# First shift and scale of a two-block transformer: one route for all feature tiles, as rows on TensorE in four column groups

## The chip, the cores and the metric

The kernel runs on one core of one Trainium2 chip. The metric is device time of one launch in microseconds. It is an fp32 kernel of batch 1 with 256 tokens and 1024 features, so nearly all of its 224 MB of traffic is weights, read once.

## The reference, cut to what matters

Two transformer blocks run one after the other. The change touches only the very first step of the first one: a modulated norm of the tokens `x` (256 of them, the stream s = 0) and of the context tokens `ctx` (256, the stream s = 1), and the projection `w_in` behind it.

```python
sc, scc = silu(c), silu(c_ctx)                       # one vector of 1024 for each stream
mod   = split(sc  @ w_mod[0] + b_mod[0], 6)           # shift1, scale1, gate1, shift2, scale2, gate2
mod_c = split(scc @ w_mod[0][:, :6*D] + b_mod[0], 6)
hn = rms_norm(ctx, g_norm1[0]) * (1 + mod_c[1]) + mod_c[0]
xn = rms_norm(x,   g_norm1[0]) * (1 + scale1)   + shift1
p, pc = xn @ w_in[0], hn @ w_in[0]                    # 1024 -> 1536
```

So shift1 and scale1 are two products of a 1024-vector with a 1024x2048 slice of `w_mod` (8 MB), for two streams that share the weights. No projection of the first layer can begin on a feature tile before shift and scale of that tile are known. The other four parts of `mod`, and all of the second layer's, are needed later and are worked out in the background.

## The kernel before, in words

**Layout.** Activations lie features on partitions: `XC` holds eight feature tiles k = 0 to 7 of 128 features by 512 columns (256 of x, 256 of ctx). Every large product is made of three matmuls on operands split into a high part (a cast to fp32r) and a low part (the remainder): `mm3` issues hi*hi (L273), lo*hi (L274) and hi*lo (L275). Activations are split into `AH` and `AL`, weights into `wh` (a cast on ACT, L243) and `wl` (a subtraction on DVE, L245; for the second half tile of all it is on Pool, by `SPH`).

**The weight stream.** Weights come in half tiles of 128x1024 f32 (512 KB) in a fixed order, `halves`. `dma_to(i)` issues loads up to half i on SP's queue into a ring of four `raw` buffers (L231); `split_to(i)` splits up to half i into a ring of four `wh`/`wl`; `done(...)` moves the stream on. `ld["lim"]` holds the stream back at the start. Halves 0 and 1 hold w_in's rows for k = 0 to 3 of the first four output tiles, halves 2 and 3 those for k = 4 to 7.

**The first stage.** The four output tiles `p_c` (four PSUM banks, 96 matmuls of 512 columns over the eight k) are accumulated k by k in `in0_k(k)`: scale and shift a tile (into `n0`, the profile's `n`), cast to `AH`, subtract for `AL`, then 12 matmuls. The rms factor of each column comes from squares on ACT (L309 to L314), adds on DVE (L315), matmuls with a vector of ones (`p_ss`, L440), a power on Pool (L299), and four transposes that spread it over the partitions (`p_rb`, L444, the tile `rb`).

Shift and scale reach `modv` by two routes:

- Tiles k = 0 to 3 (`KP = 4`): the columns are packed on the host as `wmod0`, eight loads of 512 KB (`rawm`, ring of `WRB = 4`, L425). 16 fp32 matmuls of 512 columns (L431), with the two silu vectors `scf` as a 128x2 stationary operand, give two rows `p_mod`; the rows are copied (`row`, L456) and transposed in pieces back to partitions (`p_modt`, L459); four adds and two scalings on DVE give `modv` (L464, L466).
- Tiles k = 4 to 7: `st_tile` loads a transposed tile of w_mod (`wms`, 512 KB, L491, ring of `WSB = 5`) for each of scale and shift. DVE multiplies it by `scb[:, 0]` with a sum along the row (L494), Pool multiplies it by `scb[:, 1]` (L493), ACT sums that product (L496), and a small DVE operation adds the bias (L499 for scale, L501 for shift). `scb` is the silu vectors spread over the partitions by 16 transposes (`p_scb`, L372, copied out at L373). It is used later too, by `mod_bg`, which works out the remaining parts in the background (L402, L404).

**Order.** SP's instructions stand in the order in which the program writes them. Those of the other engines are put in order by a planner that simulates the timeline at build time, so an instruction can be placed ahead of work that stands before it in the program; each engine then runs its own list strictly in order. Such a piece is `cdg`, 16 diagonal matrices that ACT makes for the convolution of the first layer (L570). After the first stage come `p_q` and the rest of the projection (L289 to L291), and the buffers of the first stage are closed (`sctx.close()`); the loads of the next pool (`sm`, L528) wait for that. Three fp32 products further on serve as comparison below: `p_fa` (L761, Fourier mixer), and `p_o` (L734) and `p_bo` (L1213), the products with V in the attention of the first and second block, where two heads write to PSUM partitions 0 to 63 and 64 to 127 in turn, each with a stationary operand of 64 columns.

Of the kernel before, what the change touches and what calls it, by code (L numbers as in the profile page):

```python
# [31 lines left out]
D = 1024  # L32
# [11 lines left out]
WRB, WSB, N0B = 4, 5, 2  # L44
KP = 4
XAT = (0, 1, 1, 2)
RWP, XR0 = 0, 2
# [107 lines left out]
def tile_kernel(ctx, tc, xin, pk_d, rows_d, lc_d, bc_d, wmod0, wmod, win, wout, wfi, wfo, wsm, win2, wproj, wout2,  # L155
# [206 lines left out]
    scf = cpool.tile([128, KT, 2], F32, name="scf")  # L362
# [5 lines left out]
    for s in range(2):  # L368
        for a in range(2):
            p = psm("p_scb")  # L370
            for k in range(4):
                PE.transpose(p[:, 128 * k:128 * k + 128], scf[:, 4 * a + k, s:s + 1].to_broadcast([128, 128]), ident)  # L372
            (S.copy if a else V.tensor_copy)(scb[:, s, 512 * a:512 * a + 512], p)  # L373
# [45 lines left out]
    nj = KP // 2  # L419
    ps = [pmm("p_mod") for _ in range(nj)]  # L420
    raws = []
    for k in range(KT):
        raw = spool.tile([128, 256 * KP], F32, tag="wr", name="rawm", bufs=WRB)
        raws.append(raw)
        SP.dma_start(raw, wmod0[k])  # L425
        for i, at in enumerate(XAT):
            if at == k:
                SP.dma_start(XC[:, 2 * i:2 * i + 2], xin[:, 2 * i:2 * i + 2])
    for k in range(KT):
        for j in range(nj):  # L430
            PE.matmul(ps[j][:2], scf[:, k, :], raws[k][:, 512 * j:512 * j + 512], start=k == 0, stop=k == KT - 1)  # L431
# [3 lines left out]
    dma_to(2)  # L435
    ld["lim"] = 2
    p = psm("p_ss")
    for i in range(4):
        for n, ss in enumerate(ss_t["ss"]):
            PE.matmul(p[:, i:i + 1], ss[:, 128 * i:128 * i + 128], ones, start=n == 0, stop=n == 1)  # L440
    r = rsqrt(p[:, :4], 4, 1.0 / D, True)
    rb = psm("p_rb")
    for i in range(4):
        PE.transpose(rb[:, 128 * i:128 * i + 128], r[:, i:i + 1].to_broadcast([128, 128]), ident)  # L444
    bm1 = cpool.tile([128, KT], F32, name="bm1")
    V.tensor_scalar(bm1, P("bmod0", 8, 8), 1.0, None, op0=OP.add)
    xr = [None] * KT
    for k in range(0, XR0, 2):
        x2 = spool.tile([128, 2, 512], F32, tag="wr", name="xr", bufs=WRB)
        for i in range(2):  # L450
            V.tensor_tensor(x2[:, i], XC[:, k + i], rb, op=OP.mult)
            xr[k + i] = x2[:, i]
# [60 lines left out]
    for k in range(KT):  # L513
        in0_k(k)
# [977 lines left out]
```

## Time and profile before

| | |
|---|---|
| median of three runs | 1382.05 us (1381.72 to 1387.13) |
| the profiled execution's own time | 1382.44 us |
| its span, first to last instruction | 1380.7 us |
| mean granted TensorE clock | 0.987 of full speed |
| busy share of the span: PE, DVE, ACT, POOL | 97%, 67%, 45%, 21% |
| HBM traffic | 221 MB read, mean 161 GB/s |

The profiled execution lies 0.4 us above the median and 1.7 us above its own span. The busy share of PE counts modelled ends of pipelined matmuls, so it isn't TensorE at its peak. PE is matmul, PEld weight loads, DVE VectorE, ACT ScalarE, POOL GpSimd, SP the engine that issues most loads. An fp32 matmul appears as two records, an fp32r matmul or a transpose as one.

### The profile page before, as it was taken

What the parts mean: (1) busy time and instruction counts of PE and PEld (TensorE: products, weight loads), DVE (VectorE), ACT (ScalarE), POOL (GpSimd) and SP (SyncE); (2) the same over time, 40 slices, a digit from 0 to 9 for tenths busy, and PEclk for the clock granted to TensorE, in tenths of its full rate; (3) what the DMA queues carried; (4) which work ended last, traced back from release to release, by engine and by line L of the source; (5) the groups of instructions that cost most, each with busy time, mean ns of one, the idle gap of its engine ahead of it and who ended that gap; (6) DMA issues with size and microseconds to landing.
All of it is one profiled execution on the core that took longest, in us unless ns stands there. A gap on an engine that the chain in (4) does not pass through costs nothing.

```text
span 1380.7 us, 23081 instructions
## 1 busy us (share of the span) xinstructions
PE 1336.6 (97%) x9000; PEld 1190.3 (86%) x9000; DVE 921.3 (67%) x1597; ACT 616.5 (45%) x1030; POOL 284.6 (21%) x302
## 2 busy tenths in 40 slices
PE   6699999999999999999999999999999999999997
PEld 2595668888888888889799999999999999999997
DVE  4987999899883333349676666666555657755553
ACT  5533533423232322335565554455665455544452
POOL 2524535134420000123430000110200002322211
PEclk9799999999999999999999999999999999999999
DMA  8442453477874222344135555665335244545463
GB/s 324 138 129 75 168 169 122 159 266 252 307 282 152 92 92 67 102 139 135 51 116 190 183 184 154 183 245 185 108 120 174 105 146 176 179 172 183 155 198 107
DMA packets 66477, 223.77 MB, mean 162 GB/s; under 512 B 7488, under 2 KB 8640, under 8 KB 66368
## 3 DMA queue, kind: packets, MB, share of 16 engines
q1 hardware_dynamic: 53824, 178.16, 38.3%
q10 hardware_dynamic: 12080, 42.50, 8.9%
q0 software_dynamic: 464, 1.64, 0.3%
q8 instruction: 70, 1.15, 0.3%
q14 instruction: 39, 0.32, 0.1%
HBM read 221.22 MB, written 1.05 MB: 161 GB/s over the span
## 4 chain that ended last, share of the span: by engine, by line
PE 89%; DVE 6%; issue 2%; ACT 1%; POOL 1%; DMA 1%; SPq 0%; DVEq 0%; POOLq 0%; ACTq 0%
PE p_dn L273 6%; PE p_dn L275 6%; PE p_dn L274 6%; PE p_ua L273 4%; PE p_ua L274 4%; PE p_ug L274 4%; PE p_ua L275 4%; PE p_ug L275 4%; PE p_ug L273 4%; PE p_wo L273 2%; PE p_wo L274 2%; PE p_wo L275 2%; PE p_bq L289 2%; PE p_bq L290 2%; PE p_bq L291 2%; PE p_ga L275 2%
## 5 line engine op out<-in xcount | busy, mean ns | idle before, releaser
L245 DVE TENSOR_TENSOR wl<-raw,wh 128x1024 fp32r<-128x1024 f32 (+2 forms) x340 | 390.0, 1149 | 280.6 <-ACT wh L243 280.0
L243 ACT CAST wh<-raw 128x1024 fp32r<-128x1024 f32 (+1 forms) x344 | 332.0, 973 | 314.4 <-PE p_dn L274 90.5
L275 PE MATMUL p_dn<-HH,wl 128*128 128x256 f32 (+1 forms) x550 | 171.7, 312 | 0.5 <-DVE wl L245 0.5
L273 PE MATMUL p_dn<-HH,wh 128*128 128x256 f32 (+1 forms) x550 | 171.8, 313 | 0.0
L274 PE MATMUL p_dn<-HL,wh 128*128 128x256 f32 (+1 forms) x550 | 171.6, 312 | 0.0
L315 POOL TENSOR_TENSOR ss<-ss,sq 128x256 f32<-128x256 f32 (+1 forms) x43 | 49.2, 1144 | 435.0 <-ACT sq L314 290.4
L274 PE MATMUL p_ua<-AL,wh 128*128 128x258 f32 (+2 forms) x368 | 121.8, 331 | 3.4 <-DVE AL L341 3.4
L275 PE MATMUL p_ug<-AH,wl 128*128 128x258 f32 (+2 forms) x368 | 121.9, 331 | 0.0
L273 PE MATMUL p_ua<-AH,wh 128*128 128x258 f32 (+2 forms) x368 | 121.9, 332 | 0.0
L274 PE MATMUL p_ug<-AL,wh 128*128 128x258 f32 (+2 forms) x368 | 121.8, 331 | 0.0
L273 PE MATMUL p_ug<-AH,wh 128*128 128x258 f32 (+2 forms) x368 | 121.7, 331 | 0.0
L275 PE MATMUL p_ua<-AH,wl 128*128 128x258 f32 (+2 forms) x368 | 121.6, 330 | 0.0
L275 PEld LDWEIGHTS p_dn<-HH,wl 128*128 128x128 f32 x550 | 104.3, 190 | 6.7 <-DVE wl L245 0.7
L273 PEld LDWEIGHTS p_dn<-HH,wh 128*128 128x128 f32 x550 | 104.3, 190 | 6.2 <-ACT wh L243 0.2
L274 PEld LDWEIGHTS p_dn<-HL,wh 128*128 128x128 f32 x550 | 104.3, 190 | 6.1
L404 DVE SCALAR_TENSOR_TENSOR wm<-wm,scb 128x1024 f32<-128x1024 f32 x80 | 99.9, 1252 | 12.0 <-DMA wm<-in_wmod 11.3
L274 PEld LDWEIGHTS p_ua<-AL,wh 128*128 128x128 f32 x368 | 69.4, 188 | 10.9 <-DVE AL L341 3.8
L273 PEld LDWEIGHTS p_ug<-AH,wh 128*128 128x128 f32 x368 | 69.2, 188 | 7.3
L275 PEld LDWEIGHTS p_ua<-AH,wl 128*128 128x128 f32 x368 | 69.3, 188 | 7.1
L274 PEld LDWEIGHTS p_ug<-AL,wh 128*128 128x128 f32 x368 | 69.4, 188 | 7.0
L273 PEld LDWEIGHTS p_ua<-AH,wh 128*128 128x128 f32 x368 | 69.2, 188 | 7.1
L275 PEld LDWEIGHTS p_ug<-AH,wl 128*128 128x128 f32 x368 | 69.3, 188 | 7.0
(376 smaller groups left out, 3397.4 us busy)
## 6 DMA issues: line engine op xcount, KB each, us to landing
raw<-in_wfi SPq DMA_DIRECT2D x88, 512.0 KB, 3.8
raw<-in_win SPq DMA_DIRECT2D x84, 512.0 KB, 3.9
wm<-in_wmod ACTq DMA_DIRECT2D x80, 512.0 KB, 4.5
raw<-in_wgu SPq DMA_DIRECT2D x44, 512.0 KB, 3.7
raw<-in_wout SPq DMA_DIRECT2D x24, 512.0 KB, 3.7
raw<-in_wfo SPq DMA_DIRECT2D x32, 384.0 KB, 3.1
raw<-in_wfo SPq DMA_DIRECT2D x32, 320.0 KB, 3.3
raw<-in_wdn SPq DMA_DIRECT2D x16, 384.0 KB, 3.1
```

Of the source, the lines that this page charges most:

```text
L243: S.copy(h[:, :n], raw[:, :n])
L245: (G if every and j % every == 0 else V).tensor_tensor(lo[:, :n], raw[:, :n], h[:, :n].bitcast(F32), op=OP.subtract)
L273: PE.matmul(ps, w[0], a[0], start=first, stop=False, **kw)
L274: PE.matmul(ps, w[0], a[1], start=False, stop=False, **kw)
L275: PE.matmul(ps, w[1], a[0], start=False, stop=last, **kw)
L289: PE.matmul(ps, a[0], w[0], start=k == 0, stop=False)
L290: PE.matmul(ps, a[0], w[1], start=False, stop=False)
L291: PE.matmul(ps, a[1], w[0], start=False, stop=k == KT - 1)
L315: (eng or G).tensor_tensor(ss[0][:, cs], ss[0][:, cs], sq[:, :n], op=OP.add)
L404: V.scalar_tensor_tensor(w, w, 1.0, scb[:, 0], op0=OP.mult, op1=OP.mult, accum_out=modv[:, l, part, 0, k:k + 1])
```

## The change

All eight feature tiles now go over TensorE, in four pairs of tiles (`mod_pair(g)`). The host packs `wmod0` as 4 pairs by 4 loads of 512 KB, each load with two of the eight contraction tiles and, for each, the pair's 512 columns (256 of shift, 256 of scale). The 512 columns are cut in four: column group c of the array, 32 columns wide, makes the products of columns 128c to 128c+127, into PSUM partitions 32c to 32c+31. For that `scf` is padded with zeros from 2 to 32 columns. So a pair is 32 fp32 matmuls of 128 columns, then one copy of 128x128, one transpose, and four small DVE operations that serve both streams. `st_tile` is gone, with its eight products on DVE, eight on Pool and eight sums on ACT; so are `bm1` and the fused form in `in0_k` (scale and rms in one DVE operation for each stream): now one DVE product by the rms factor for both streams, then scale and shift on ACT, for all k.

`XC` is loaded first, ahead of all of `wmod0`. `LOADS = "mhmhmm"` gives the order behind it on SP: a pair (m), two weight halves (h), a pair, two halves, two pairs; `in0_k` follows as soon as its pair and its halves have been issued. The ring of `rawm` has 8 buffers instead of 4. The spreading of `scb` (`scb_fill`) stands at the end of the stage in the program.

```diff
@@ -41,10 +41,8 @@
 UW = T + 2 * POOL_PAD
 
 RAW, WB, EV, NT, PTB, PEB, WMB = 4, 4, 4, 2, 2, 2, 4
-WRB, WSB, N0B = 4, 5, 2
-KP = 4
-XAT = (0, 1, 1, 2)
-RWP, XR0 = 0, 2
+WRB, XRB, N0B = 8, 4, 2
+LOADS = "mhmhmm"
 NPE = 8
 CVD, FOD = 0.9, 1
 BG0, BG1 = 2.4, 2.0
@@ -359,18 +357,21 @@
     lctx = ctx.enter_context(ExitStack())
     lpool = lctx.enter_context(tc.tile_pool(name="lp", bufs=1))
     modv = cpool.tile([128, 2, 6, 2, KT], F32, name="modv")
-    scf = cpool.tile([128, KT, 2], F32, name="scf")
+    scf = cpool.tile([128, KT, 32], F32, name="scf")
+    G.memset(scf, 0.0)
     for s in range(2):
         S.activation(scf[:, :, s], P("c", 8 * s, 8), AF.Silu)
     scb = lpool.tile([128, 2, D], F32, name="scb")
     lc = lpool.tile([128, LC_W], F32, name="lc")
 
-    for s in range(2):
-        for a in range(2):
-            p = psm("p_scb")
-            for k in range(4):
-                PE.transpose(p[:, 128 * k:128 * k + 128], scf[:, 4 * a + k, s:s + 1].to_broadcast([128, 128]), ident)
-            (S.copy if a else V.tensor_copy)(scb[:, s, 512 * a:512 * a + 512], p)
+    def scb_fill():
+
+        for s in range(2):
+            for a in range(2):
+                p = psm("p_scb")
+                for k in range(4):
+                    PE.transpose(p[:, 128 * k:128 * k + 128], scf[:, 4 * a + k, s:s + 1].to_broadcast([128, 128]), ident)
+                (S.copy if a else V.tensor_copy)(scb[:, s, 512 * a:512 * a + 512], p)
 
     def mv(l, part, s):
         return modv[:, l, part, s]
@@ -416,102 +417,82 @@
 
     sctx = ctx.enter_context(ExitStack())
     spool = sctx.enter_context(tc.tile_pool(name="st", bufs=1))
-    nj = KP // 2
-    ps = [pmm("p_mod") for _ in range(nj)]
-    raws = []
-    for k in range(KT):
-        raw = spool.tile([128, 256 * KP], F32, tag="wr", name="rawm", bufs=WRB)
-        raws.append(raw)
-        SP.dma_start(raw, wmod0[k])
-        for i, at in enumerate(XAT):
-            if at == k:
-                SP.dma_start(XC[:, 2 * i:2 * i + 2], xin[:, 2 * i:2 * i + 2])
-    for k in range(KT):
-        for j in range(nj):
-            PE.matmul(ps[j][:2], scf[:, k, :], raws[k][:, 512 * j:512 * j + 512], start=k == 0, stop=k == KT - 1)
+    for i in range(4):
+        SP.dma_start(XC[:, 2 * i:2 * i + 2], xin[:, 2 * i:2 * i + 2])
     new_ss(True)
     for k in range(KT):
         sq_acc(k, slice(0, 512), k == 0, V)
-    dma_to(2)
-    ld["lim"] = 2
-    p = psm("p_ss")
-    for i in range(4):
-        for n, ss in enumerate(ss_t["ss"]):
-            PE.matmul(p[:, i:i + 1], ss[:, 128 * i:128 * i + 128], ones, start=n == 0, stop=n == 1)
-    r = rsqrt(p[:, :4], 4, 1.0 / D, True)
-    rb = psm("p_rb")
-    for i in range(4):
-        PE.transpose(rb[:, 128 * i:128 * i + 128], r[:, i:i + 1].to_broadcast([128, 128]), ident)
-    bm1 = cpool.tile([128, KT], F32, name="bm1")
-    V.tensor_scalar(bm1, P("bmod0", 8, 8), 1.0, None, op0=OP.add)
-    xr = [None] * KT
-    for k in range(0, XR0, 2):
-        x2 = spool.tile([128, 2, 512], F32, tag="wr", name="xr", bufs=WRB)
-        for i in range(2):
-            V.tensor_tensor(x2[:, i], XC[:, k + i], rb, op=OP.mult)
-            xr[k + i] = x2[:, i]
-    pt = psm("p_modt")
-    for j in range(nj):
+
+    def first_rms():
+        p = psm("p_ss")
+        for i in range(4):
+            for n, ss in enumerate(ss_t["ss"]):
+                PE.matmul(p[:, i:i + 1], ss[:, 128 * i:128 * i + 128], ones, start=n == 0, stop=n == 1)
+        r = rsqrt(p[:, :4], 4, 1.0 / D, True)
+        rb = psm("p_rb")
+        for i in range(4):
+            PE.transpose(rb[:, 128 * i:128 * i + 128], r[:, i:i + 1].to_broadcast([128, 128]), ident)
+        return rb
+
+    def mod_pair(g):
+
+        p = psm("p_mod")
+        for q in range(4):
+            raw = spool.tile([128, 2, 512], F32, tag="wr", name="rawm", bufs=WRB)
+            SP.dma_start(raw.rearrange("p i n -> p (i n)"), wmod0[g, q])
+            for i in range(2):
+                k = 2 * q + i
+                for c in range(4):
+                    PE.matmul(p[32 * c:32 * c + 32, :128], scf[:, k], raw[:, i, 128 * c:128 * c + 128], start=k == 0,
+                              stop=k == KT - 1)
         row = wk.tile([128, 512], F32, tag="ev", name="row", bufs=EV)
-        S.copy(row[:2], ps[j][:2])
-        for b in range(4):
-            o = 2 * (4 * j + b)
-            PE.transpose(pt[:, o:o + 2], row[:2, 128 * b:128 * b + 128], ident[:2, :2])
-    ptv = pt[:, :4 * KP].rearrange("p (a k s) -> p a k s", a=2, s=2)
-    for part in (1, 0):
-        for s in range(2):
-            d = modv[:, 0, part, s, 0:KP]
-            V.tensor_tensor(d, ptv[:, part, :, s], P("bmod0", part * 8, KP), op=OP.add)
+        S.copy(row[:, :128], p[:, :128])
+        pt = psm("p_modt")
+        PE.transpose(pt[:, :128], row[:, :128], ident)
+        v = pt[:, :128].rearrange("p (a k x) -> p a x k", a=2, x=32)
+        for part in (1, 0):
+            d = modv[:, 0, part, :, 2 * g:2 * g + 2]
+            V.tensor_tensor(d, v[:, part, 0:2], P("bmod0", part * 8 + 2 * g, 2)[:, None, :].to_broadcast([128, 2, 2]),
+                            op=OP.add)
             if part == 1:
-                V.scalar_tensor_tensor(d, d, 1.0, P("g1_0", 0, KP), op0=OP.add, op1=OP.mult)
+                V.scalar_tensor_tensor(d, d, 1.0, P("g1_0", 2 * g, 2)[:, None, :].to_broadcast([128, 2, 2]), op0=OP.add,
+                                       op1=OP.mult)
+
     n_ = "in0"
     ps4 = [pmm("p_c") for _ in range(4)]
 
     def in0_k(k):
+        x = spool.tile([128, 512], F32, tag="xr", name="xr", bufs=XRB)
+        V.tensor_tensor(x, XC[:, k], rb, op=OP.mult)
         t = spool.tile([128, 512], F32, tag="n0", name="n0", bufs=N0B)
-        if xr[k] is None and k % 2 == 0:
-            x2 = spool.tile([128, 2, 512], F32, tag="wr", name="xr", bufs=WRB)
-            xr[k], xr[k + 1] = x2[:, 0], x2[:, 1]
         for s in (0, 1):
             c = slice(256 * s, 256 * s + 256)
-            if k < XR0:
-                S.activation(t[:, c], xr[k][:, c], AF.Identity, bias=mv(0, 0, s)[:, k:k + 1],
-                             scale=mv(0, 1, s)[:, k:k + 1])
-            else:
-                V.scalar_tensor_tensor(xr[k][:, c], XC[:, k, c], mv(0, 1, s)[:, k:k + 1], rb[:, c], op0=OP.mult,
-                                       op1=OP.mult)
-                S.activation(t[:, c], xr[k][:, c], AF.Identity, bias=mv(0, 0, s)[:, k:k + 1])
+            S.activation(t[:, c], x[:, c], AF.Identity, bias=mv(0, 0, s)[:, k:k + 1], scale=mv(0, 1, s)[:, k:k + 1])
         S.copy(AH[:, k, 0:512], t)
         V.tensor_tensor(AL[:, k, 0:512], t, AH[:, k, 0:512].bitcast(F32), op=OP.subtract)
         for m in range(4):
             mm3(ps4[m], wk256(n_, m // 2, k, 128 * (m % 2)), act(k, slice(0, 512)), k == 0, k == KT - 1)
 
-    def st_tile(part, k):
-        w = spool.tile([128, D], F32, tag="wms", name="wms", bufs=WSB)
-        SP.dma_start(w, wmod[0, 8 * part + k])
-        jg = spool.tile([128, D], F32, tag="jgs", name="jgs", bufs=2)
-        G.tensor_tensor(jg, w, scb[:, 1], op=OP.mult)
-        V.scalar_tensor_tensor(w, w, 1.0, scb[:, 0], op0=OP.mult, op1=OP.mult,
-                               accum_out=modv[:, 0, part, 0, k:k + 1])
-        S.activation(jg, jg, AF.Copy, accum_out=modv[:, 0, part, 1, k:k + 1])
-        d = modv[:, 0, part, :, k]
-        if part == 1:
-            V.tensor_scalar(d, d, bm1[:, k:k + 1], P("g1_0", k), op0=OP.add, op1=OP.mult)
+    ld["lim"] = 0
+    rb = None
+    n_mod, n_in = 0, 0
+    for c in LOADS:
+        if c == "m":
+            mod_pair(n_mod)
+            n_mod += 1
+            if rb is None:
+                rb = first_rms()
         else:
-            V.tensor_scalar(d, d, P("bmod0", k), None, op0=OP.add)
-
-    split_to(2)
-    for i in range(2 * (KT - KP)):
-        if i == RWP:
-            ld["lim"] = WB
-            split_to(WB)
-        st_tile(1 - i % 2, KP + i // 2)
+            ld["lim"] += 2
+            split_to(ld["lim"])
+        while n_in < min(2 * n_mod, 2 * ld["split"]):
+            in0_k(n_in)
+            n_in += 1
     ld["lim"] = 10 ** 6
     SP.dma_start(rows, bass.AP(tensor=rows_d.tensor, offset=rows_d.offset, ap=[[0, 128], [1, 512]]))
     SP.dma_start(lc, lc_d)
     dma_to(WB + RAW)
-    for k in range(KT):
-        in0_k(k)
+    scb_fill()
     sctx.close()
 
 
@@ -1432,7 +1413,7 @@
     rows += [inp["sgu_ln_g_2"][0], inp["sgu_ln_b_2"][0]]
     a["rows"] = np.concatenate(rows)
     a["lc"], a["bc"] = _shape_consts()
-    a["wmod0"] = inp["w_mod"][0][:, :2048].reshape(8, 128, 2, 1024)[..., :128 * KP].reshape(8, 128, 256 * KP)
+    a["wmod0"] = inp["w_mod"][0][:, :2048].reshape(4, 2, 128, 2, 4, 256).transpose(4, 0, 2, 1, 3, 5).reshape(4, 4, 128, 1024)
     a["wmod"] = inp["w_mod"].transpose(0, 2, 1).reshape(2, 48, 128, 1024)
     qcols = np.concatenate([h * 64 + dh for h in (0, 2, 1, 3)])
     kcols = 256 + np.concatenate([h * 64 + dh for h in (0, 1)])
```

## Rows read from the trace of the kernel before

**Rows 1.** Busy tenths in 40 equal slices of the span (34.5 us each), from the page.
```profile
PE   6699999999999999999999999999999999999997
...
DVE  4987999899883333349676666666555657755553
```

**Rows 2.** Waits of PE, 0 to 75 us: engine, line, releaser: total us, times, longest.
```profile
PE p_c L273 <- ACT AH L484: 9.9, 2, 8.4
PE p_c L274 <- DVE AL L485: 6.8, 4, 3.1
```

**Rows 3.** Busy time by stretch (us, records), granted clock, DMA share, GB/s.
```profile
30.00:75.30 45.30, 29.99 (x96) 22.09 (x96) 39.67 (x51) 23.42 (x44) 25.62 (x20) 0.77 0.45 153
75.30:140.00 64.70, 62.34 (x335) 47.64 (x334) 55.23 (x91) 20.97 (x49) 23.86 (x24) 0.98 0.30 100
```

**Rows 4.** The chain that ended last, 30 to 76 us: start us, us, what.
```profile
by line: DMA wms<-in_wmod 28.6%; DVE wms L494 22.5%; issue 14.0%; DVE modv L501 8.7%; DVE xr L481 7.3%; PE p_c L274 6.4%; DVE modv L499 6.3%; DVE AL L485 5.8%; DVE wl L245 5.2%; DVE modv L466 4.8%; PE p_c L275 4.8%; PE p_c L273 2.0%; ACT sg
...
69.81 0.43 PE p_c L275
...
72.51 0.94 PE p_c L273 x4
...
74.86 0.25 PE p_c L274
```

**Rows 5.** Groups by line and form, 0 to 76 us: busy us, mean ns, idle before.
```profile
L493 POOL TENSOR_TENSOR jgs<-wms,scb 128x1024 f32<-128x1024 f32 x8 | 24.0, 3014 | 7.4 <-ACT jgs L496 6.9 <-DMA wms<-in_wmod 0.4
...
L494 DVE SCALAR_TENSOR_TENSOR wms<-wms,scb 128x1024 f32<-128x1024 f32 x8 | 11.9, 1487 | 0.0
...
L243 ACT CAST wh<-raw 128x1024 fp32r<-128x1024 f32 x8 | 8.4, 1044 | 15.1 <-DMA raw<-in_win 10.8 <-PE p_c L274 4.2
...
L483 ACT ACTIVATE n<-xr,modv 128x256 f32<-128x256 f32 x12 | 5.5, 502 | 12.3 <-DVE modv L501 6.8 <-DVE AL L485 5.3
L484 ACT CAST AH<-n 128x512 fp32r<-128x512 f32 x8 | 4.9, 607 | 0.1
...
L451 DVE TENSOR_TENSOR xr<-XC,p_rb 128x512 f32<-128x512 f32 x2 | 1.3, 680 | 0.0
```

**Rows 6.** One tile's operations, `modv`, 0 to 76 us: ns min/median/max.
```profile
L464 DVE TENSOR_TENSOR modv<-p_modt,pk x4: 144/146/148, 29.7 to 29.9; 128x4 f32<-128x4 f32 x4
...
L499 DVE TENSOR_SCALAR modv<-modv,bm,pk x4: 275/1308/2361, 38.6 to 64.9; 128x2 f32<-128x2 f32 x4
```

**Rows 7.** Waits of SP's queue, 0 to 76 us: total us, times, longest.
```profile
SPq L491 <- DVE wms L494: 22.2, 3, 12.8
```

**Rows 8.** DMA throughput in 40 slices of 1.9 us, 0 to 76 us.
```profile
GB/s 4 303 356 390 414 418 418 414 364 119 345 222 356 414 420 412 410 101 0 4 140 144 0 0 263 43 292 139 400 410 414 252 0 0 0 0 0 49 332 266
```

**Rows 9.** Timeline of the start: start us, us, engine, instruction, count.
```profile
3.63 4.78 ACT L570 ACTIVATE cdg<-ident,pk 128x128 f32<-128x128 f32 x16 [0.68 <-POOL pk L197]
...
13.78 0.61 ACT L311 ACTIVATE ssl<-XC 128x512 f32<-128x512 f32 x1
...
15.27 1.88 PE L431 MATMUL p_mod<-rawm,scf 128*2 128x512 f32 x4
...
19.09 1.04 POOL L299 TENSOR_TENSOR rs_r<-rs_v,mhalf 128x4 f32<-128x4 f32 x1 [15.49 <-DVE rs_v L298]
...
23.98 0.65 PE L444 MATMUL p_rb<-ident,rs_r 128*128 128x128 f32 x4
```

**Rows 10.** Timeline of PE: fp32 matmul records, stationary operand 128 or 64 columns wide.
```profile
123.35 1.03 PE L761 MATMUL p_fa<-lc,U 128*128 128x256 f32 x4
...
994.50 0.87 PE L1213 MATMUL p_bo<-bPT,vt 128*64 128x256 f32 x6
...
142.48 0.66 PE L734 MATMUL p_o<-pT,VT 128*64 128x128 f32 x8
```

**Rows 11.** One tile's operations, `p_o`: ns min/median/max.
```profile
L742 ACT COPY awo<-p_o x12: 254/265/274, 141.2 to 701.1; 128x128 f32<-128x128 f32 x12
```

**Rows 12.** The longest wait of PE from 75 to 300 us, as in rows 2.
```profile
PE p_ua L274 <- DVE AL L341: 3.4, 2, 2.1
```

## The prediction, made before the changed kernel had run

> **What bounds the kernel now.** The page's busy tenths come first: PE is at nine tenths from the third slice on and lower only in the first two, 69 us [rows 1]. What can be won cheaply lies there, and that is where the change is. The windows say how much: from 30.0 to 75.3 us PE shows 96 matmul records, exactly the 96 of `p_c`, DVE is busy 39.7 of 45.3 us, the granted clock is 0.77 and the DMA share 0.45 [rows 3]. So neither matmuls nor loads set this stretch. The waits of PE name what does: 9.9 us for `AH`, 6.8 us for `AL`, both products of shift and scale [rows 2]. The chain that ended last agrees: from 30 to 76 us it runs over the `wms` loads (28.6%), the `wms` products on DVE (22.5%) and the small `modv` operations; `p_c` is under a seventh of it [rows 4]. The loads are no bound of their own: SP's queue waits 22.2 us for DVE to hand back a `wms` buffer [rows 7], and the throughput falls from 410 to near 0 and to 140 GB/s while it does [rows 8].
>
> Why DVE is so slow stands in the group table. Its eight `wms` products cost 11.9 us, Pool's eight 24.0 us [rows 5]. The small operations of L499, two elements for each partition, take 275 ns at best and 2361 ns at worst [rows 6]; the long ones stand beside a running Pool product. The last `p_c` matmul of this stage ends at 74.86 + 0.25 = 75.1 us [rows 4]. Behind it PE's longest single wait up to 300 us is 2.1 us and its waits for one releaser sum to 3.4 us at most [rows 12]: no event there has a time of its own, so I let everything behind 75 us move as a block. The change is then worth what it moves the end of `p_c`.
>
> **What goes.** DVE loses 11.9 us of `wms` products and the slow small ones, Pool all 24.0 us, ACT eight sums. In their place DVE has 8 products by the rms factor at 0.68 us [rows 5] and about four small operations for each pair at 0.146 us [rows 6], some 8 us together: DVE is no bound any more. One Pool operation stays, the low part of weight half 1.
>
> **Loads.** The stage moves the same bytes: 4 loads of `XC`, 16 of w_mod, 4 weight halves, 24 of 512 KB, 12.6 MB. Summed over the 1.9 us slices, 0.58 MB have come by 3.8 us, 2.8 MB by 9.5 us, and from there 0.79 MB a slice [rows 8]. In the new order that puts `XC` complete at 7.8 us, pair 0 at 12.9, the first two halves at 15.4, pair 1 at 20.4, the next halves at 23.0, pair 2 at 28.0 and pair 3 at 33.0 us. Pairs 2 and 3 reuse the eight buffers of pairs 0 and 1; SP may then stand behind PE, but `rows`, `lc` and the next halves behind them are needed only after `p_c`.
>
> **Start of p_c.** The rms factor decides it. ACT does 16 `cdg` pieces until 8.4 us, then the squares until 13.78 + 0.61 = 14.4 us [rows 9]. If that order stays, the earlier `XC` buys nothing. The power on Pool began 4.7 us later; 1.9 us of that are the four `p_mod` records that stand between the `p_ss` ones [rows 9], leaving 2.8. Then 1.04 for the power, 0.65 for the transposes [rows 9], 0.68 for the product, two activations at 0.50 and a cast at 0.61 [rows 5]: 14.4 + 2.8 + 1.0 + 0.7 + 0.7 + 1.0 + 0.6 = 21.2. I take 21. If the squares go ahead of `cdg`, the first halves bound it: 15.4, two casts at 1.04, low parts: about 18.
>
> **p_c itself.** 96 matmuls. At the full clock four take 0.94 us, 0.235 each; at the lower level one takes 0.43 [rows 4]. All at full clock is 22.6 us, all at the lower 41. PE will be less idle than before, yet in bursts; I add 2 us, ten matmuls at the lower level.
>
> **The four pairs on PE.** A pair is 32 matmuls, 64 records, of 128 columns. No four-wide group runs in the trace, but two-wide ones do. A full-width record of 256 columns takes (1.03 - 0.38)/3 = 0.217 us; in two column groups six records take 0.87, (0.87 - 0.38)/5 = 0.098 us each [rows 10] (the 0.38 is the last record's modelled length). So two groups do overlap. At 128 columns two groups need (0.66 - 0.27)/7 = 0.055 us a record [rows 10], where a quarter of a 512-column `p_mod` record ((1.88 - 0.60)/3 = 0.43 us) [rows 9] is 0.107. For four groups the bounds are 0.027 (twice the overlap again, 1.7 us a pair) and 0.107 (none, 6.8 us). I take 0.055, 3.5 us a pair: the count of instructions, not the columns, may be what is left, and p_o is the nearest row.
>
> [...]
>
> **Between pairs.** `p_c` of a pair needs the last load's 8 matmuls (16 records, 0.9 us), the row copy 0.27 [rows 11], a transpose of about 0.2 (four take 0.65) [rows 9], three of the small DVE operations 0.45 [rows 6], two activations 1.0 and a cast 0.6 [rows 5], and some five hand-offs, about 0.5 by my estimate from the gaps in [rows 9]: 3.9 us. Each engine runs its list in order; if the planner puts a pair's last matmuls behind all of the `p_c` before, PE stands for 3 us of this, and the next pair's other loads (2.6 us) fit into that time. Three boundaries: 12 us. If all interleaves, only the records are left, 3 x 3.5 = 10.5 us, or 5.2 at 0.027. If nothing does, 3 x (3.5 + 3.0) = 20.
>
> **Sum.** 21 + 22.6 + 2 + 12 = 57.6 us for the end of `p_c` against 75.1: 17.5 us less. The spreading of `scb` is 16 transposes and four copies; four transposes cost 0.65 [rows 9], so about 2 us if it lands on PE between `p_c` and `p_q`. I put it at 0: the planner placed `cdg`, far later work, at 3.6 us [rows 9], and PE is idle early and at the boundaries. Without that cover the end comes 2 us later. The clearing of `scf` precedes the silu on a Pool that is idle until the vectors have landed, also 0. The profiled execution's own time, 1382.4 us, gives 1382.4 - 17.5 = 1364.9; the median is 0.4 lower, so 1365.
>
> **Rivals.**
> - Loads bind: four groups overlap fully and the lists interleave. End of p_c 18 + 22.6 + 5.2 = 46, and pair 3 (33.0 + 3.9 + two tiles 5.6 = 42.5) allows it. Gain 29, 1353 us. For it: the 410 GB/s [rows 8]. Against it: the 55 ns. Chance 0.15.
> - Four groups don't overlap: 6.8 us a pair. A boundary holds 1.7 + 3.0 and 2.1 of the next pair's records that no longer fit, 20 us for three; start at 22, 22 + 22.6 + 3 + 20 = 68, gain 7, 1375 us. Against it: two groups do overlap [rows 10]. Chance 0.11, half of it on each side of 0.5%.
> - Slower: `p_c` in four bursts, each at the lower clock because PE waits ahead of each, and no record hidden: 21 + 41 + 3 x (7 + 3) = 92, 17 us later, 1399 us. For it: the clock of 0.77 between 30 and 75 us [rows 3]. It decides only from 82 us on: with all of `p_c` at the lower level the boundaries must cost over 20 us; with boundaries of 12 the end is 74. Chance 0.06.
> - No change: `p_c` ends earlier but the next stretch doesn't, because DVE, busy 55.2 of 64.7 us there [rows 3], or a later load holds it to the old pace. Against it: that DVE work (conv taps) itself starts from `p_c`, and [rows 12]. 1380 us, chance 0.08.
> - The forecast, 1365 us: 0.60, its own range 1358 to 1371.
>
> **Range and chances.** A measurement of this kernel can tell 0.5%, 6.9 us, from no change. Faster: 0.60 + 0.15 + half of 0.11 = 0.80; within: 0.14; slower: 0.06. From the loads' bound to just past the case without overlap, 1353 to 1377, leaves out the last two cases and the far tails, under 2 in 10.
>
> **What would show it.** Right: the last `p_c` matmul at 52 to 64 us, the first near 21; the 128*32 records 0.05 to 0.06 us apart; no wait of SP for DVE; small `modv` operations near 0.15 us; DMA near 410 GB/s up to 33 us with short dips. Wrong: records at 0.107 us; a granted clock at its lower level for most of `p_c`; waits of PE for `AH` above 3 us at every pair; or a later first `p_c` because the planner placed `p_rb` behind pair 1. If `p_c` ends 17 us earlier and the whole does not, the block behind it was not free to move.

## The result and the profile after

The changed kernel takes 1368.22 us (median of four runs, 1367.64 to 1371.9) against 1382.43 us for the kernel before, four runs beside them: ratio 0.9896, 95% interval 0.9868 to 0.9924, 14.2 us or 1.0% faster. The profiled execution took 1368.16 us, its span is 1366.5 us, its mean granted clock 0.994 (for the first 28 us of it, see under the experiment "Warm PE").

Busy tenths of the page, slices of 34.2 us; they answer to [rows 1]:

```profile
PE   5999999899999999999999999999999999999997
...
DVE  4597998999873333369577666665655657655554
```

The second slice of PE is now full. Next the windows of the two stretches that answer to [rows 3], `p_c` and the 65 us behind it (columns as there):

```profile
28.60:59.20 30.60, 30.39 (x243) 23.00 (x243) 12.96 (x25) 15.24 (x29) 2.57 (x12) 1.00 0.58 219
59.20:124.00 64.80, 62.44 (x335) 47.78 (x334) 55.21 (x90) 21.05 (x50) 23.72 (x24) 0.97 0.30 102
```

The stage of `p_c` takes 30.6 us instead of 45.3, PE has no gaps to speak of in it, DVE is busy 13 us instead of 40, and the granted clock is 1.00 instead of 0.77. The stretch behind it is nearly what it was: the same 335 records, 62.4 us of PE and 55.2 of DVE. The waits of PE from 0 to 60 us, which answer to [rows 2]:

```profile
PE p_mod L446 <- ACT ssl L309: 12.4, 1, 12.4
PE p_rb L434 <- POOL rs_r L297: 1.9, 1, 1.9
PE p_c L271 <- ACT AH L471: 0.8, 1, 0.8
```

The 16.7 us for `AH` and `AL` have shrunk to 0.8. What is left is the start. (`p_mod` reads `rawm`, not `ssl`: a wait is put down to the event that came last, and in a second profile of this kernel the same wait, 11.9 us, stands against the `rawm` load.) The timeline of PE, Pool and ACT up to the first `p_c`, then PE's own pieces within `p_c` (against [rows 9]):

```profile
12.36 2.27 PE L446 MATMUL p_mod<-rawm,scf 128*32 128x128 f32 x32 [12.36 <-ACT ssl L309]
...
16.10 1.08 PE L446 MATMUL p_mod<-rawm,scf 128*32 128x128 f32 x16 [0.18 <-DMA rawm<-in_wmod]
17.90 0.43 PE L430 MATMUL p_ss<-ones,ss 128*128 128x1 f32 x2
...
19.77 2.34 POOL L243 TENSOR_TENSOR wl<-raw,wh 128x1024 fp32r<-128x1024 f32 x1 [15.96 <-ACT wh L241]
...
22.07 1.04 POOL L297 TENSOR_TENSOR rs_r<-rs_v,mhalf 128x4 f32<-128x4 f32 x1
...
23.17 1.11 PE L434 MATMUL p_rb<-ident,rs_r 128*128 128x128 f32 x4 [1.85 <-POOL rs_r L297]
24.21 3.64 PE L446 MATMUL p_mod<-rawm,scf 128*32 128x128 f32 x64
25.05 2.08 ACT L470 ACTIVATE n<-xr,modv 128x256 f32<-128x256 f32 x4 [5.35 <-DVE xr L466]
28.63 1.21 PE L271 MATMUL p_c<-AH,wh 128*128 128x512 f32 x4 [0.77 <-ACT AH L471]
...
35.51 1.74 PE L446 MATMUL p_mod<-rawm,scf 128*32 128x128 f32 x56
43.58 1.93 PE L446 MATMUL p_mod<-rawm,scf 128*32 128x128 f32 x58
49.69 1.47 PE L373 MATMUL p_scb<-ident,scf 128*128 128x128 f32 x12
...
58.91 0.40 PE L273 MATMUL p_c<-AH,wl 128*128 128x512 f32 x1
```

Three readings. First, `p_ss` stands in PE's list behind all of pair 0, whose last load is worked at 16.1 to 17.2 us; `p_ss` ends at 21.3 us and the small DVE operation behind it at 21.5; then Pool is busy with the low part of weight half 1 until 22.1 us, so the power starts at 22.07; then ACT makes four activations and a weight cast before the first `AH` is done. `p_c` begins at 28.6 us. Second, 56 records of a pair take 1.74 us: (1.74 - 0.27)/55 = 0.027 us each, four column groups side by side. Third, `p_scb` fell into `p_c`. The last `p_c` matmul ends at 58.91 + 0.25 = 59.2 us, against 75.1. (Ends of `p_c` are good to 0.1 us here, since the ends of matmuls are modelled.)

Two one-tile rows of `modv`, against [rows 6], and the throughput in slices of 1.9 us, against [rows 8]:

```profile
L455 DVE TENSOR_TENSOR modv<-p_modt,pk x8: 151/157/164, 18.1 to 50.0; 128x4 f32<-128x4 f32 x8
...
L458 DVE SCALAR_TENSOR_TENSOR modv<-modv,pk x4: 163/164/165, 18.3 to 50.1; 128x4 f32<-128x4 f32 x4
```

```profile
GB/s 4 301 280 326 360 407 423 420 399 414 412 416 407 410 403 410 412 405 411 416 410 388 149 4 0 9 0 0 0 197 310 319 278 274 75 9 0 0 73 203
```

The small operations are all at their short time, and the loads run at about 410 GB/s without a hole up to 41 us.

**Where 16 became 14.** `p_c` ends 15.9 us earlier; the execution is 14.3 us shorter (1382.44 - 1368.16). I cut each trace at the first matmul of `p_q`, `p_wo`, `p_ua`, `p_dn` of the first layer and so on, and compared the lengths of the stages (us; the stages left out differ by 0.2 or less):

| profile | `p_q` starts | to `p_wo` | to `p_ua` | to `p_dn` | second layer: `p_q` to `p_wo` | `p_ua` to `p_dn` |
|---|---|---|---|---|---|---|
| before | 75.8 | 94.6 | 70.7 | 128.3 | 53.6 | 127.1 |
| after | 59.8 | 94.5 | 70.6 | 130.0 | 52.8 | 128.5 |

Two stages give back 1.7 and 1.4 us, one gains 0.8. The first: in both kernels PE waits ahead of `p_ua` for `AL` (after here, before in [rows 12]):

```profile
PE p_ua L272 <- DVE AL L339: 3.7, 2, 2.1
```

Behind this wait of after, the window of 30 us shows a granted clock of 0.95 and 125 matmul records; the same stretch of before, 16.2 us later, has 1.00 and 131:

```profile
253.80:283.80 30.00, 30.00 (x125) 24.23 (x124) 27.79 (x46) 9.29 (x14) 10.44 (x12) 0.95 0.75 267
```

```profile
270.00:300.00 30.00, 30.00 (x131) 24.27 (x130) 27.83 (x46) 8.88 (x13) 10.63 (x13) 1.00 0.73 262
```

Much the same wait was followed by a fall of the clock in one profile and not in the other. The second, 1.4 us in the second layer, has no wait and no lower clock: at 1.00 in both, 40 us hold 333 matmul records after and 337 before. Its cause stays open.

### The profile page after: what moved, and what is told of

Read it like the earlier page. It is cut to its first block, busy times and chain, and to the rows that moved or that the text cites. A ratio compares the mean times of both kernels' runs of the same rounds, so it can differ in the third digit from the quotient of the medians.

```text
span 1366.5 us, 23461 instructions
## 1 busy us (share of the span) xinstructions
PE 1329.0 (97%) x9220; PEld 1193.9 (87%) x9220; DVE 893.6 (65%) x1572; ACT 608.3 (45%) x1016; POOL 262.1 (19%) x295
## 4 chain that ended last, share of the span: by engine, by line
PE 90%; DVE 4%; POOL 2%; ACT 1%; DMA 1%; issue 1%; SPq 0%; POOLq 0%; DVEq 0%; ACTq 0%
PE p_dn L271 6%; PE p_dn L273 6%; PE p_dn L272 6%; PE p_ua L272 5%; PE p_ua L273 5%; PE p_ua L271 5%; PE p_ug L272 5%; PE p_ug L273 5%; PE p_ug L271 4%; PE p_wo L271 2%; PE p_wo L272 2%; PE p_wo L273 2%; PE p_bq L287 2%; PE p_bq L289 2%; PE p_bq L288 2%; PE p_ga L273 2%
## 5 line engine op out<-in xcount | busy, mean ns | idle before, releaser
L405 DVE SCALAR_TENSOR_TENSOR wm<-wm,scb 128x1024 f32<-128x1024 f32 x80 | 99.0, 1242 | 10.1 <-DMA wm<-in_wmod 9.9
## 6 DMA issues: line engine op xcount, KB each, us to landing
rawm<-in_wmod SPq DMA_DIRECT2D x16, 512.0 KB, 10.1
```

The costliest lines, as they stand in the source:

```text
L405: V.scalar_tensor_tensor(w, w, 1.0, scb[:, 0], op0=OP.mult, op1=OP.mult, accum_out=modv[:, l, part, 0, k:k + 1])
```

## Experiments

The theory: the kernel before was bound at the start by DVE and Pool, the new stage by its late start and by PE itself, and the end of `p_c` is nearly all that counts. The rivals: the loads, or the overlap of the column groups alone, or an event further back, set the time. Ratios are to the kernel before on the same chip: four runs of the kernel (where nothing else is said) and 7 to 18 of the kernel before. The new order of the loads and the deeper ring of `rawm` were not run apart from the rest.

**One column group.** The changed kernel without the groups.

```diff
-                for c in range(4):
-                    PE.matmul(p[32 * c:32 * c + 32, :128], scf[:, k], raw[:, i, 128 * c:128 * c + 128], start=k == 0,
-                              stop=k == KT - 1)
+                PE.matmul(p[:32], scf[:, k], raw[:, i], start=k == 0, stop=k == KT - 1)
...
+            for c in range(4):
+                PE.transpose(pt[:, 32 * c:32 * c + 32], row[:32, 128 * c:128 * c + 128], ident[:32, :32])
```

> The changed kernel without column groups: a pair is 8 fp32 matmuls of 512 columns on one 32-wide group. Theory (PE's list is what is left: from the first p_c matmul at 28.6 us to the last at 59.2 it stands almost nowhere): 16 records at 0.43 us are 6.9 us a pair against 1.74, so pairs 2 and 3 cost 5.1 us more each, pair 1, ahead of p_c, about 3, pair 0 about 2: 1368 + 12 to 15 = 1380 to 1383. Rival (loads or the chain from rows to shift and scale bind, the records hide in waits): at most 4 us more, 1372 or less.

Measured: 1388.65 us, ratio 1.0041 (1.0026 to 1.0056): slower than the kernel before. Its timeline of PE:

```profile
12.13 9.22 PE L445 MATMUL p_mod<-rawm,scf 128*32 128x512 f32 x16 [12.13 <-DMA rawm<-in_wmod]
...
26.34 8.75 PE L445 MATMUL p_mod<-rawm,scf 128*32 128x512 f32 x16
35.02 1.20 PE L271 MATMUL p_c<-AH,wh 128*128 128x512 f32 x4
...
41.16 3.19 PE L445 MATMUL p_mod<-rawm,scf 128*32 128x512 f32 x7
```

At the full clock (the `p_c` records just ahead follow each other at 0.23 us) a record of 512 columns takes (3.19 - 0.60)/6 = 0.43 us; the four of 128 columns that replace it take 4 x 0.027 = 0.11, a quarter. `p_c` starts 6.4 us later (35.0), partly because pair 1 now fills PE in front of it, and ends at 76.7, 17.5 us later than with the groups: without them the new stage is no better than the old one. The direction was expected, the price was too low: 20 us, not 12 to 15. Since this kernel has the new order of the loads and the deeper ring as well, these alone are not the gain either.

**No loads for three pairs.** Pairs 1 to 3 use the four tiles of pair 0 again, so 6.3 MB are not read.

```diff
-            raw = spool.tile([128, 2, 512], F32, tag="wr", name="rawm", bufs=WRB)
-            SP.dma_start(raw.rearrange("p i n -> p (i n)"), wmod0[g, q])
+            if g == 0:
+                raw = spool.tile([128, 2, 512], F32, tag="wr", name="rawm", bufs=WRB)
+                SP.dma_start(raw.rearrange("p i n -> p (i n)"), wmod0[g, q])
+                kept.append(raw)
+            raw = kept[q]
```

> The changed kernel with the loads of pairs 1 to 3 left out: they use pair 0's four tiles again, so shift and scale of tiles 2 to 7 are not the reference's; 6.3 MB less is loaded in the stage. Theory (PE's list binds, and its start hangs on the rms factor): first p_c matmul at 28 to 29 us, total 1366 to 1369. Rival (loads bind the stage as they fill the queue until 41 us): p_c ends 8 us or more earlier, 1360 or less.

Measured: 1369.62 us, 0.9902 (0.9887 to 0.9917); `p_c` from 28.4 to 58.6 us. Half of the stage's traffic is gone and the end of `p_c` moves 0.6 us, no more than between two profiles of the changed kernel (below): the loads of pairs 1 to 3 are not the bound. Pair 0 was still loaded, so the run says nothing of it.

**`scb` first.** The spreading of `scb` is put back to the head of the stage.

```diff
     dma_to(WB + RAW)
-    scb_fill()
     sctx.close()
...
+    scb_fill()
     sctx = ctx.enter_context(ExitStack())
```

> The changed kernel with scb_fill at the head of the stage, where it stood before. Theory (PE stands almost nowhere between 28.6 and 59.2 us): the 16 transposes, 1.75 us in the chain there, leave it: p_c ends 1.5 to 2 us earlier, 1366 to 1367. Rival (waits for the next pair take their place): p_c ends within 0.5 us of 59.2, 1368.

Measured: 1369.39 us, 0.9897 (0.9881 to 0.9914); `p_c` from 28.5 to 58.5. The 1.8 us of `p_scb` left the middle of `p_c`, and this came in its place (PE's waits):

```profile
PE p_c L271 <- ACT AH L472: 2.1, 2, 1.3
```

The end moves 0.6 us, not 1.5 to 2, and as little as between two profiles of the changed kernel: `p_scb` had for the most part filled a time in which PE would have waited for `AH`.

**`p_ss` first.** Pair 0's matmuls from its second load on are issued behind `p_ss`.

```diff
+        ss_t["mm"] = getattr(ins, "ins", ins)             # last p_ss matmul
...
+                with (tc.issue_after(ss_t["mm"]) if g == 0 and q > 0 else ExitStack()):
...
-            mod_pair(n_mod)
-            n_mod += 1
             if rb is None:
                 rb = first_rms()
+            mod_pair(n_mod)
+            n_mod += 1
```

> The changed kernel with the p_ss matmuls ahead of pair 0's on PE (first_rms before mod_pair(0), loads 1 to 3 of pair 0 queued behind p_ss). Theory (p_c starts at 28.6 instead of the predicted 21 because p_ss stands in PE's list behind all of pair 0, whose last load's matmuls run at 16.1 to 17.2 us): p_ss at about 14, p_rb at about 18, first p_c at 24 to 25, total 1363 to 1366. Rival (weight halves and pair 0 set the start anyway, or what is gained at the start is lost to waits for later pairs): 1367 to 1369.

Measured: 1371.75 us, 0.9921 (0.9906 to 0.9936); `p_c` from 30.1 to 60.3. The theory fell here. The timeline of PE:

```profile
15.03 0.59 PE L430 MATMUL p_ss<-ones,ss 128*128 128x1 f32 x2 [15.03 <-DVE ss L313]
...
20.45 1.12 PE L435 MATMUL p_rb<-ident,rs_r 128*128 128x128 f32 x4 [1.85 <-POOL rs_r L297]
21.49 3.64 PE L448 MATMUL p_mod<-rawm,scf 128*32 128x128 f32 x64
...
26.50 3.48 PE L448 MATMUL p_mod<-rawm,scf 128*32 128x128 f32 x64
30.08 1.20 PE L271 MATMUL p_c<-AH,wh 128*128 128x512 f32 x4
```

`p_rb` does come 2.7 us earlier, but now the records of two pairs run behind it, 128 where the changed kernel has 64, the first 64 of them (3.64 - 0.42)/63 = 0.051 us apart, twice the 0.027 of later ones (0.42 is the last record's modelled length), and `p_c` starts 1.5 us later than without the edit. An order that frees one thing moves another behind it.

**The kernel before, with column groups for its own rows only**, and **the kernel before, with Pool's products on DVE**.

```diff
-        for j in range(nj):
-            PE.matmul(ps[j][:2], scf[:, k, :], raws[k][:, 512 * j:512 * j + 512], start=k == 0, stop=k == KT - 1)
+        for c in range(4):
+            PE.matmul(ps[32 * c:32 * c + 32, :256], scf[:, k, :], raws[k][:, 256 * c:256 * c + 256], start=k == 0,
+                      stop=k == KT - 1)
```

> The kernel before with one part of the change alone: its rows for tiles 0 to 3 in four column groups (scf padded to 32 columns, 4 matmuls of 256 columns in place of 2 of 512). st_tile, the order of loads and all else stay. Theory (before, the products on DVE and Pool set the end of p_c; PE's 13.7 us of rows lie in idle time): 1379 to 1383. Rival (the column groups are the gain): 1374 or less.

```diff
-        G.tensor_tensor(jg, w, scb[:, 1], op=OP.mult)
+        V.scalar_tensor_tensor(jg, w, 1.0, scb[:, 1], op0=OP.mult, op1=OP.mult,
+                               accum_out=modv[:, 0, part, 1, k:k + 1])
...
-        S.activation(jg, jg, AF.Copy, accum_out=modv[:, 0, part, 1, k:k + 1])
```

> The kernel before with the Pool products of st_tile moved to DVE, as a second product with a sum; the eight sums on ACT go. Theory (DVE stands still beside a running Pool product: between 28 and 70 us L466, L499 and L501 lose about 11 us against their shortest, L494, L485 and L245 about 5 more): DVE takes 8 x 1.3 = 10.4 us of work and loses some 16 of standing, p_c ends about 5 us earlier, 1375 to 1379, and no small operation of L499 or L501 is over 0.4 us. Rival (the long small operations are waits for data and have nothing to do with Pool): DVE is the bound and gets 10 us more, 1390 or more.

Measured: with groups 1384.45 us (10 runs) against 1384.58 (18 runs), 1.0003 (0.9990 to 1.0015), `p_c` ends at 72.2 us; with DVE alone 1378.91 us (9 runs), 0.9961 (0.9948 to 0.9973), `p_c` ends at 72.4 us. One-tile rows of `modv` of the second, against [rows 6]:

```profile
L499 DVE TENSOR_SCALAR modv<-modv,bm,pk x4: 271/272/277, 42.5 to 62.0; 128x2 f32<-128x2 f32 x4
...
L466 DVE SCALAR_TENSOR_TENSOR modv<-modv,pk x2: 145/147/149, 31.6 to 32.8; 128x4 f32<-128x4 f32 x2
```

L499 had 275 to 2361 ns, now 271 to 277, although DVE does twice as many products. So the long ones were the neighbour's, Pool's. The time fell by 5.7 us, as forecast, but not by the way forecast: `p_c` ends 2.7 us earlier, not 5, in a profile that is the slowest of the nine (1381.47 us). The groups by themselves take 2.9 us off the end of `p_c` and nothing off the median. Their profile (1383.80 us) gave the 2.9 us back behind `p_q`, above all in the stage from `p_ua` to `p_dn`: 131.5 us against 128.3, at a granted clock that falls to 0.83 over 20 us. So the groups alone are not the gain, nor are the rows without them (the first experiment): the change needs both. In neither of these two runs does the whole follow the end of `p_c` to better than 3 us.

**An earlier start.** `p_ss` first as above; `cdg` issued behind the last square; the low part of half 1 on DVE, so that Pool is free for the power. A second kernel has `scb` first as well.

```diff
-SPL, SPH = {"wo1": 3}, (1,)
+SPL, SPH = {"wo1": 3}, ()
...
+                with (tc.issue_after(ss_t["last"]) if l == 0 else ExitStack()):   # ahead of the cdg activations
```

> The changed kernel with the start brought forward: p_ss ahead of pair 0 on PE, the cdg pieces on ACT behind the squares, the low part of weight half 1 on DVE instead of Pool. Theory (start hangs on the rms factor): first p_c at 20 to 22 us; then the loads of pair 3, which land at about 38, hold the last two tiles, so p_c ends at 50 to 53 and the total is 1359 to 1363. Rival (first p_c is held by the weight halves or the clock and the list simply moves): first p_c at 25 or later, 1365 or more.

> As the run before with scb_fill at the head as well. Theory (PE's list still binds with the early start): 1.5 to 2 us less than that run. Rival (loads bind by then): the same as that run within 0.5 us.

Measured: 1370.63 us, 0.9906 (0.9888 to 0.9923), `p_c` from 26.2 to 61.0; with `scb` first 1371.71 us, 0.9914 (0.9897 to 0.9931), 26.3 to 60.5. The start is 2.4 us earlier and the end 1.8 later than in the changed kernel. The 20 to 22 us forecast for the start were missed and the rival's figures held; `scb` first brought nothing here either. PE, ACT and PE's waits of the first of the two:

```profile
17.31 1.12 PE L436 MATMUL p_rb<-ident,rs_r 128*128 128x128 f32 x4 [1.38 <-POOL rs_r L297]
18.35 3.18 PE L449 MATMUL p_mod<-rawm,scf 128*32 128x128 f32 x64
...
23.52 2.07 ACT L473 ACTIVATE n<-xr,modv 128x256 f32<-128x256 f32 x4 [1.65 <-DVE modv L461]
...
PE p_c L271 <- ACT AH L474: 5.0, 3, 1.9
```

The rms factor is ready early, at 18.4 us, but pair 0's 64 records now stand behind it, so shift and scale come last. Further on the planner now ends a pair's matmuls behind all of the `p_c` before, so the chain of row copy, transpose, `modv`, activation and cast stands open three times, 1.7 us each.

**Warm PE.** 14 fp32 matmuls of 256 columns on data that has already landed run on PE before pair 0; nothing reads them.

```diff
+    pw = psm("p_warm")
+    for i in range(14):
+        PE.matmul(pw[:32, :256], scf[:, i % KT], pk[:, 0:256], start=True, stop=True)
```

> The changed kernel with 14 fp32 matmuls of 256 columns ahead of the stage on PE (zero-padded scf by columns of pk, a PSUM tile that nobody reads). Theory (part of the late start is the clock: PE idles until 12.3 us, and at the lower level the p_ss records are 0.21 us apart and the pair records 0.053, where the full clock shows 0.11 and 0.027): p_ss and p_rb take 2 us less, first p_c at 26 to 27 instead of 28.6, total 1 to 2.5 us less than the changed kernel. Rival (pair 1's records, ACT's list or the halves hold the first p_c there anyway): the same within 0.5 us.

Measured: 1368.39 us, 0.9881 (0.9858 to 0.9903), `p_c` from 25.5 to 59.2. Two windows (the last three columns are granted clock, DMA share, GB/s) and two records of this kernel:

```profile
12.00:18.00 6.00, 4.27 (x78) 2.81 (x76) 3.01 (x7) 2.26 (x5) 0.00 (x0) 1.00 1.02 416
20.00:26.00 6.00, 5.08 (x69) 4.14 (x70) 3.92 (x7) 3.20 (x7) 3.21 (x2) 0.50 1.01 404
...
16.10 0.64 PE L449 MATMUL p_mod<-rawm,scf 128*32 128x128 f32 x16 [0.63 <-DMA rawm<-in_wmod]
...
21.97 3.64 PE L449 MATMUL p_mod<-rawm,scf 128*32 128x128 f32 x64
```

The 16 records at 16.1 us take 0.64 us at a granted clock of 1.00; the same ones took 1.08 in the changed kernel. The 64 at 22 us take 3.64 us at 0.50, as long as in the changed kernel. There the clock column reads 1.00 up to 28 us all the same, so it does not show the lower level at the start of that profile; where this text speaks of the lower level ahead of `p_c`, it goes by the spacing of the records. `p_ss` is over by 19.1 us instead of 21.3, the start is 3.1 us earlier, and 3.1 us of waits for `AH` take it all back: the whole is the same as that of the changed kernel beside it (1368.09), as the rival said.

**The chain between pairs covered.** The earlier start, and `p_c` of a pair's second tile issued behind the next pair's transpose; a second kernel has the warm PE too. The changed kernel itself ran beside them again.

```diff
+        with (tc.issue_after(tr[k // 2 + 1]) if k % 2 and k < KT - 1 else ExitStack()):
             for m in range(4):
                 mm3(ps4[m], wk256(n_, m // 2, k, 128 * (m % 2)), act(k, slice(0, 512)), k == 0, k == KT - 1)
...
-        while n_in < min(2 * n_mod, 2 * ld["split"]):
+        while n_in < min(2 * n_mod - (n_mod < 4), 2 * ld["split"]):
```

> The run with the early start, with the order on PE set by hand: the p_c matmuls of a pair's second tile stand behind the next pair's transpose, so that the next pair's shift and scale are worked out under them. Theory (in the early run p_c began 2.4 us sooner and that was lost in 5.0 us of waits for AH, because the transposes of the rows stood behind all of the pair before): waits for AH under 2 us in all, p_c ends at 56 to 58, total 3 to 5 us less than the early run. Rival (the waits come from loads of later pairs): waits for AH stay near 5 us and the total is the same.

> As the run before, with the 14 matmuls ahead on PE. Theory (clock and order are both left over at the start): first p_c at 22 to 24, end of p_c at 52 to 55, total 1361 to 1364. Rival (loads of pairs 2 and 3, which land at about 33 and 38 us, bind by then): end of p_c not before 56.

> The changed kernel once more, beside the three others on the same chip: 1367 to 1370, p_c from 28.6 to 59.2. A p_c end that moves by more than 0.5 us, or a stage behind it whose length moves by over 1.5 us, would say how much of the differences between these runs is the execution and not the edit.

Measured:

| kernel | median | ratio (95%) | `p_c` | `p_wo` to `p_ua` | `p_ua` to `p_dn` |
|---|---|---|---|---|---|
| early, covered | 1369.45 | 0.9887 (0.9866 to 0.9907) | 26.0 to 56.4 | 72.6 | 129.8 |
| early, covered, warm | 1367.96 | 0.9876 (0.9856 to 0.9895) | 25.5 to 55.9 | 72.6 | 130.1 |
| the changed kernel again | 1368.09 | 0.9880 (0.9857 to 0.9903) | 28.2 to 58.6 | 70.6 | 128.4 |

The cover does what it should: the waits for `AH` fall from 5.0 to 1.4 us and the end of `p_c` moves 4.6 us against the uncovered early start, 2.2 to 2.7 against the changed kernel beside them. The whole gains nothing, where 3 to 5 us and 1361 to 1364 us had been forecast. The changed kernel's second profile has the end of `p_c` 0.6 us earlier than its first and the stage from `p_ua` to `p_dn` 1.6 us shorter: differences of that size between single profiles are the execution's and not the edit's. Two microseconds go in the stage from `p_wo` to `p_ua`. DVE's timeline there, first after, then the covered kernel, and the latter's waits of PE between 198 and 228 us:

```profile
205.56 1.65 DVE L878 SCALAR_TENSOR_TENSOR XC<-p_wo,modv,XC 128x256 f32<-128x256 f32 x4
207.13 1.21 DVE L243 TENSOR_TENSOR wl<-raw,wh 128x1024 fp32r<-128x1024 f32 x1
208.26 2.31 DVE L405 SCALAR_TENSOR_TENSOR wm<-wm,scb 128x1024 f32<-128x1024 f32 x1
...
210.50 0.47 DVE L878 SCALAR_TENSOR_TENSOR XC<-p_wo,modv,XC 128x256 f32<-128x256 f32 x1
```

```profile
202.92 1.65 DVE L886 SCALAR_TENSOR_TENSOR XC<-p_wo,modv,XC 128x256 f32<-128x256 f32 x4
204.48 1.21 DVE L243 TENSOR_TENSOR wl<-raw,wh 128x1024 fp32r<-128x1024 f32 x1
205.61 2.32 DVE L406 SCALAR_TENSOR_TENSOR wm<-wm,scb 128x1024 f32<-128x1024 f32 x1
207.86 2.30 DVE L404 SCALAR_TENSOR_TENSOR jg<-wm,scb 128x1024 f32<-128x1024 f32 x1
...
210.10 0.87 DVE L886 SCALAR_TENSOR_TENSOR XC<-p_wo,modv,XC 128x256 f32<-128x256 f32 x2
```

```profile
PE p_wo L271 <- DVE XC L886: 1.0, 2, 0.8
PE p_ss L325 <- POOL ss L314: 0.7, 1, 0.7
```

Both lists run 2.65 us apart up to the `wm` product of 2.3 us. There the covered kernel has a second background product, also 2.3 us long, ahead of the update of `XC`, which comes 0.4 us earlier than in after, not 2.65. PE stands for it and for `p_ss`. That the order of DVE's list did this is read from the traces; no kernel with only that product moved was run.

## Why the prediction was right, and where it was off

1365 us were predicted and 1368.2 measured: the mechanism and the direction held, but the sum came out by errors that partly cancel. By its own steps:

- **What bounds the kernel before.** Right as far as the runs show. Taking Pool's products away and nothing else frees the small operations and brings 5.7 us, of which 2.7 are seen in the end of `p_c`; faster rows alone bring nothing in the median. (One reading of [rows 1] is loose: the last slice of PE, too, is below nine tenths, at seven.)
- **The start of `p_c`, 21 us: 28.6.** The mis-sized term. The squares ended at 13.3 us, 1.1 earlier than assumed. From there to the power I allowed 2.8 us, and the prediction named the risk of PE's list only for `p_rb` behind pair 1. The adds on DVE were done at 14.9; `p_ss` stood behind pair 0's last load until 17.9; it took 3.4 us, 0.21 us a record, where records 0.11 us apart, as in the kernel before, would take 1.8: PE had stood idle up to 12.4 us, while before it had worked from 3.0 us on, and in the kernel with the warm PE, where it works from 4.7 us on, the records are 0.11 us apart again; Pool's weight half cost another 0.5. The power began at 22.07, 4.9 us later than the 17.2 of my chain. The transposes took 1.11 us at the lower level instead of 0.65, and ACT's list had four activations, a weight cast and the cast of `AH` where I counted two activations and the cast of `AH`: 2.0 us more. 4.9 + 0.5 + 2.0 = 7.4 against the chain's 21.2, 7.6 against the 21 that I took.
- **The records, 0.055 us: 0.027** at the full clock, the lower bound. A pair costs 1.7 to 1.9 us there, 3.6 at the lower level.
- **The boundaries, 12 us, and the clock's 2 us.** From first to last `p_c` matmul it is 30.5 us: 22.5 for the 96 matmuls, 4.2 for the records of pairs 2 and 3 (pair 1's ran before `p_c`), 0.6 for transposes, 1.8 for `p_scb`, some 1.4 of gaps. I had 22.6 + 2 + 12 = 36.6. The clock was 1.00 throughout `p_c` (the lower level, with pair records 0.051 us apart, struck ahead of it), and the planner did interleave the pairs, so the chain of 3 us stood open nowhere. The early kernel, with 5.0 us of waits for `AH`, shows what it costs when it does.
- **`scb` at 0:** 1.8 us in the middle of `p_c`, but its removal brought at most 0.6.
- **The loads.** Their rate was as forecast, 410 GB/s. They landed later: the median from issue to landing of a `rawm` load is 10.1 us (6.2 in the kernel before, with its ring of four), pair 0's last load was worked at 16.1 us (12.9 forecast) and half 1 landed at 18.65 (15.4). Those of pairs 1 to 3 still bind nothing, as the kernel without them shows; pair 0's do stand in the chain of the start, since `p_ss` ran behind the records of its last load. The sign "no wait of SP for DVE" holds for the loads of w_mod: the 22.2 us of [rows 7] are gone. For the `sm` load of the next pool SP still waits 19.5 us for DVE, as it did before (18.7).
- **The sum.** 7.6 us late, 6.1 us shorter: the end of `p_c` at 59.2 instead of 57.6. That the two nearly cancel is luck.
- **The block behind moves rigidly.** Nearly: 15.9 us went in, 14.3 came out. The rest shows no second bound. In 14 profiles of this case the stage from `p_ua` to `p_dn` is 128.3 to 128.7 us long in six and 129.8 to 131.6 in eight; in the 20 us around that wait the granted clock is 1.00 in all of the six and 0.83 to 0.91 in all of the eight, and the changed kernel has been in both groups. The 1.4 us of the second layer are in every version of the changed kernel (128.5 or 128.6 us); unexplained.

**The rivals.** Loads as the bound: out. Groups that don't overlap: out, by the 0.027; and with one group the kernel is at 1388.65, above what I priced for that case, since the start suffers too. Four bursts at the lower clock: out, the clock is 1.00; but the one-group kernel ends on that side. No change because the stretch behind holds the pace: out for 14 of the 16 us; of the further 2 to 3 us of the covered kernels nothing came through.

## What to carry to other kernels

When rows times a matrix with few rows fill a 32-wide column group, four groups cost a quarter of the time here (4 x 0.027 us against 0.43); in the whole this paid only together with freeing the engine that set the stage: faster matmuls alone left the median where it was (ratio 1.0003). Price the start of a stage by the order of every engine's list, not by the chain of needs: what stands ahead in PE's, Pool's and ACT's lists, with a PE that had stood idle up to 12.4 us and then showed the `p_ss` records 0.21 us apart instead of 0.11, cost 7 us here that the chain didn't show. And where a planner orders the lists, microseconds won at the head are not yet won at the end: follow them stage by stage, and look at the clock of each before giving a change the blame.

## What the runs showed of the hardware

- fp32 matmuls of 128 columns on four column groups in turn follow each other at 27 ns a record at the full clock (granted clock 1.00 in `p_c`) and 51 ns at the lower level (granted clock 0.50 in the kernel with the warm PE); at the full clock that is a quarter of what one group of 512 columns takes for the same work (0.43 us a record).
- In the kernel before, the four DVE operations of two elements a partition that ran beside a Pool product took 1.53 to 2.36 us, the four others 0.21 to 0.28 us; without the products all eight took 0.21 to 0.28.
- The same wait of 3.7 us of PE was followed by a lower granted clock (0.91 over 20 us) in one profile of the changed kernel and not in the other (1.00).
- The clock column of a profile can read 1.00 at its start while records run at the spacing of the lower level: 64 records take 3.64 us at 1.00 in the changed kernel and 3.64 us at 0.50 in the kernel with the warm PE.
